# A rotary-embedding kernel: the first slab's load split over two DMA rings, and a second buffer for the sin products

## The chip, the cores and the metric

The kernel runs on one core of a Trainium2 chip. The metric is the device time of one execution in microseconds (us); lower is better. A verdict of faster or slower needs 2%. The profile of a kernel is one execution; its span is about 2 us below the device time.

## The reference

The input x has 16 batches of 512 positions of 16 heads of 64 numbers, all float32; cos and sin have 512 x 32 numbers.

```python
x = x.reshape(batch, seq, num_heads, head_dim)          # 16, 512, 16, 64
x1, x2 = x[..., :half_dim], x[..., half_dim:]
rotated = np.concatenate([x1 * cos - x2 * sin,
                          x1 * sin + x2 * cos], axis=-1)
```

That is 33.5 MB in and 33.5 MB out of HBM, the chip's main memory, with a few operations on each number.

## The kernel before

x is cut into 8 slabs of 2 batches. One slab is a tile in SBUF, the on-chip memory, of 128 partitions, each holding 8192 float32, so one DMA row (one partition) is 32 KB. There are 5 slab buffers. Loads are issued from SP, stores from ScalarE (ACT); each of these two has its own DMA ring, a queue of transfers for the 16 DMA engines (q1 and q10 on the pages below, 33.55 MB each). A slab is worked on in 2 passes: ScalarE casts half a slab to bf16, VectorE (DVE) makes two products and a sum, ScalarE casts the result back into the slab.

```python
slabs = ctx.enter_context(tc.tile_pool(name="slabs", bufs=slots))      # 5
tpool = ctx.enter_context(tc.tile_pool(name="tpool", bufs=3))
t2pool = ctx.enter_context(tc.tile_pool(name="t2pool", bufs=1))
# ... cut
def load(s):
    slab[s] = slabs.tile([P, W], f32, tag="slab", name="slab")
    nc.sync.dma_start(out=slab[s], in_=dram(x, s))

load(0)
# ... cut: cos and sin are loaded through GpSimd, 64 KB each
for s in range(1, slots):
    load(s)
# ... cut: the cos and sin tables are spread with four matmuls
for i, u in enumerate(passes):                 # 16 passes: (slab, half)
    if i + 1 < len(passes):
        cast(passes[i + 1])                    # ScalarE: xb <- slab
    # ... cut
    t2 = t2pool.tile([P, PW], bf16, tag="t2")
    # ... cut: t2 <- xb * sin table; xu <- xb * cos table; xu <- xu + t2  (VectorE)
    nc.scalar.copy(out=view(xs, k * PW, (1, PW)), in_=xu)
    if k == rpp // rows - 1:
        nc.scalar.dma_start(out=dram(out_flat, s), in_=xs)
        if s + slots < nslabs:
            load(s + slots)
```

Of the kernel before, what the change touches and what calls it, by code (L numbers as in the profile page):

```python
# [2 lines left out]

# [4 lines left out]


@with_exitstack  # L10
def kernel(
    ctx: ExitStack,
    tc: tile.TileContext,
    x: bass.AP,
    cos: bass.AP,
    sin: bass.AP,
    num_heads: int,
    out: bass.AP,
):
    nc = tc.nc  # L20
    P = nc.NUM_PARTITIONS

    batch, seq, dim = x.shape
    nh = num_heads
    hd = dim // nh
    half = hd // 2
    bf16 = mybir.dt.bfloat16
    f32 = mybir.dt.float32

    nb = 2  # L30
    slots = 5
    nslabs = batch // nb
    rpp = nb * seq // P
    W = rpp * dim
    SP = seq // rpp
    rows = 4
    PW = rows * dim
    TW = rpp * half

    out_flat = out.rearrange("b s h d -> b s (h d)")  # L40

    singles = ctx.enter_context(tc.tile_pool(name="singles", bufs=1))
    slabs = ctx.enter_context(tc.tile_pool(name="slabs", bufs=slots))
    tpool = ctx.enter_context(tc.tile_pool(name="tpool", bufs=3))
    t2pool = ctx.enter_context(tc.tile_pool(name="t2pool", bufs=1))
    psum = ctx.enter_context(tc.tile_pool(
        name="psum", bufs=1, space=bass.MemoryType.PSUM))


    def dram(t, s, a=0, n=W):  # L50
        return bass.AP(tensor=t.tensor, offset=t.offset + s * nb * seq * dim + a,
                       ap=[[W, P], [1, n]])


    def view(t, offset, *dims):
        return dataclasses.replace(t, offset=t.offset + offset,
                                   ap=[t.ap[0], *[list(d) for d in dims]])


    slab = {}  # L60


    def load(s):
        slab[s] = slabs.tile([P, W], f32, tag="slab", name="slab")
        nc.sync.dma_start(out=slab[s], in_=dram(x, s))  # L65


    load(0)


    TR = seq // P
    G = rpp // TR
    raw = singles.tile([P, 2 * TR * half], f32, tag="raw")
    for i, src in enumerate((cos, sin)):
        nc.gpsimd.dma_start(out=view(raw, i * TR * half, (1, TR * half)), in_=bass.AP(  # L75
            tensor=src.tensor, offset=src.offset,
            ap=[[TR * half, P], [1, TR * half]]))

    for s in range(1, slots):
        load(s)  # L80


    pick = singles.tile([P, G * P], bf16, tag="pick")
    nc.gpsimd.memset(pick, 0.0)  # L84
    for g in range(G):
        part = view(pick, g * P, (SP, P // SP), (1, SP))
        nc.gpsimd.affine_select(  # L87
            out=part, in_=part, compare_op=mybir.AluOpType.not_equal, fill=1.0,
            base=-g, pattern=[[0, P // SP], [-G, SP]], channel_multiplier=1)

    tab1 = singles.tile([P, 2 * TR * half], bf16, tag="tab1")
    nc.vector.tensor_copy(out=tab1, in_=raw)  # L92
    acc = psum.tile([P, 2 * TW], f32, tag="acc")
    for i in range(2):
        for g in range(G):
            nc.tensor.matmul(view(acc, i * TW + g * TR * half, (1, TR * half)),  # L96
                             view(pick, g * P, (1, P)),
                             view(tab1, i * TR * half, (1, TR * half)),
                             start=True, stop=True)

    tab = singles.tile([P, 2 * rpp * hd], bf16, tag="tab")
    nc.vector.tensor_copy(out=view(tab, 0, (hd, 2 * rpp), (1, half)),  # L102
                          in_=view(acc, 0, (half, 2 * rpp), (1, half)))
    nc.vector.tensor_copy(out=view(tab, half, (hd, rpp), (1, half)),  # L104
                          in_=view(acc, 0, (half, rpp), (1, half)))
    nc.vector.tensor_scalar_mul(  # L106
        out=view(tab, rpp * hd + half, (hd, rpp), (1, half)),
        in0=view(acc, TW, (half, rpp), (1, half)), scalar1=-1.0)


    xb = {}


    def cast(u):
        s, k = u
        xb[u] = tpool.tile([P, PW], bf16, tag="xb", name="xb")
        nc.scalar.copy(out=xb[u], in_=view(slab[s], k * PW, (1, PW)))  # L117



    passes = [(s, k) for s in range(nslabs) for k in range(rpp // rows)]
    cast(passes[0])
    for i, u in enumerate(passes):
        if i + 1 < len(passes):
            cast(passes[i + 1])
        s, k = u
        xs, xu = slab[s], xb.pop(u)
        t2 = t2pool.tile([P, PW], bf16, tag="t2")
        for t, a in ((t2, rpp * hd), (xu, 0)):
            nc.vector.tensor_mul(  # L130
                out=t, in0=xu,
                in1=view(tab, a + k * rows * hd, (hd, rows), (0, nh), (1, hd)))
        nc.vector.tensor_add(  # L133
            out=xu, in0=xu,
            in1=view(t2, half, (hd, rows * nh), (-half, 2), (1, half)))
# [8 lines that stand above are left out]
# [1 line left out]
_INS = ['x', 'cos', 'sin', 'num_heads']  # L145
_OUTS = [((16, 512, 16, 64), 'float32')]

_NUMBERS = {'num_heads': 16}


# [26 lines left out]
```

## Time and profile before

| | before |
|---|---|
| device time, first 3 runs | 162.83 us (162.74 to 163.21) |
| span of the profiled run | 160.8 us |
| busy: VectorE, ScalarE | 69%, 71% |
| the two hardware rings, share of 16 DMA engines | 49.3% + 48.3% |
| first slab landed | 13.2 us |
| first store issued | 34.6 us |

The page of the kernel before: the busy line, the share of the 16 DMA engines in 40 slices of the span in tenths, and the DMA queues (packets, MB, share of 16 engines' span). q1 is SP's ring, q10 is ScalarE's, q0 is GpSimd's (POOL). PE is the matrix engine and PEld its weight loads, both nearly idle here.

```profile
PE 0.6 (0%) x4; PEld 0.4 (0%) x4; DVE 111.7 (69%) x52; ACT 114.8 (71%) x33; POOL 2.3 (1%) x9
...
DMA  7999999999999999999999999999999999999993
...
q1 hardware_dynamic: 1152, 33.55, 49.3%
q10 hardware_dynamic: 1152, 33.55, 48.3%
q0 software_dynamic: 64, 0.13, 0.2%
```

The two rings together fill 97.6% of the engines' time, and only the first and last slices fall below 9 tenths. The compute engines have slack of about 30% (busy 69% and 71%). So, by these shares, a change counts only by what it does to DMA work or to the two ends.

The timeline of ScalarE, kernel before (start us, us, engine, line, operation, out<-in, count, and in brackets the idle time before it and its releaser):

```profile
0.74 1.28 ACT L117 ACT_TABLE_LOAD   x1 [0.74 <-PEq L158]
13.25 7.11 ACT L117 CAST xb<-slab 128x4096 bf16<-128x4096 f32 x2 [11.22 <-DMA slab<-in_x_dram]
23.92 3.61 ACT L137 CAST slab<-xb 128x4096 f32<-128x4096 bf16 x1 [3.56 <-DVE xb L133]
...
34.60 0.38 ACTq L139 DMA_DIRECT2D out_dram<-slab  x1
```

ScalarE waits 11.22 us for the first slab. The costliest groups of VectorE (busy us, mean ns of one, then the idle just before them) show that the single sin buffer makes nothing wait, as the sum and the cos product have 0.5 us of idle over 16 passes each:

```profile
L130 DVE TENSOR_TENSOR t<-xb,tab 128x4096 bf16<-128x4096 bf16 x16 | 36.7, 2292 | 19.4 <-ACT xb L117 18.6
L133 DVE TENSOR_TENSOR xb<-xb,t 128x4096 bf16<-128x4096 bf16 x16 | 36.7, 2292 | 0.5
L130 DVE TENSOR_TENSOR xb<-xb,tab 128x4096 bf16<-128x4096 bf16 x16 | 36.7, 2292 | 0.5
```

### The profile page before, as it was taken

Reading aid. Unit: us, or ns where it says so; the run is one execution under the profiler, and the core shown is the slowest. Engines: PE = TensorE matmul, PEld = TensorE weight load, DVE = VectorE, ACT = ScalarE, POOL = GpSimd, SP = SyncE. Lnnn points to the kernel's source line nnn. Section 1 sums busy time; section 2 is a strip of 40 time slices with the busy share of each in tenths; the row PEclk is TensorE's granted clock in tenths of the full one; section 3 lists DMA queues with packets and bytes.
Section 4 is the critical chain, followed back from the end, with each engine's and each line's share of the span. In section 5 each row is a group of like instructions: output and inputs, shape, how many; then the busy total and the mean of one; then the engine's idle time right before and its main releaser. Section 6 shows DMA issues by size and latency. Waiting matters only on the chain.

```text
span 160.8 us, 197 instructions
## 1 busy us (share of the span) xinstructions
PE 0.6 (0%) x4; PEld 0.4 (0%) x4; DVE 111.7 (69%) x52; ACT 114.8 (71%) x33; POOL 2.3 (1%) x9
## 2 busy tenths in 40 slices
PE   0010000000000000000000000000000000000000
PEld 0000000000000000000000000000000000000000
DVE  0012799999999999999997599907997079970000
ACT  3007919999999999999994999069990699926000
POOL 5000000000000000000000000000000000000000
DMA  7999999999999999999999999999999999999993
GB/s 261 408 408 416 497 391 391 505 408 367 416 391 473 440 391 456 457 391 424 489 391 424 489 391 399 514 391 391 522 391 393 489 416 399 481 424 399 481 424 139
DMA packets 2369, 67.25 MB, mean 418 GB/s; under 512 B 288, under 2 KB 288, under 8 KB 320
## 3 DMA queue, kind: packets, MB, share of 16 engines
q1 hardware_dynamic: 1152, 33.55, 49.3%
q10 hardware_dynamic: 1152, 33.55, 48.3%
q0 software_dynamic: 64, 0.13, 0.2%
q14 instruction: 1, 0.01, 0.0%
HBM read 33.69 MB, written 33.55 MB: 418 GB/s over the span
## 4 chain that ended last, share of the span: by engine, by line
DMA 47%; ACT 22%; DVE 21%; issue 0%; ACTq 0%; SPq 0%; DVEq 0%
DMA slab<-in_x_dram 26%; DMA out_dram<-slab 21%; ACT slab L137 11%; ACT xb L117 11%; DVE xb L133 7%; DVE t L130 7%; DVE xb L130 7%; ACTq L137 0%; SPq L65 0%; DVEq L130 0%
## 5 line engine op out<-in xcount | busy, mean ns | idle before, releaser
L117 ACT CAST xb<-slab 128x4096 bf16<-128x4096 f32 x16 | 57.5, 3601 | 24.8 <-DMA slab<-in_x_dram 24.8
L137 ACT CAST slab<-xb 128x4096 f32<-128x4096 bf16 x16 | 57.7, 3604 | 7.2 <-DVE xb L133 7.1
L130 DVE TENSOR_TENSOR t<-xb,tab 128x4096 bf16<-128x4096 bf16 x16 | 36.7, 2292 | 19.4 <-ACT xb L117 18.6
L133 DVE TENSOR_TENSOR xb<-xb,t 128x4096 bf16<-128x4096 bf16 x16 | 36.7, 2292 | 0.5
L130 DVE TENSOR_TENSOR xb<-xb,tab 128x4096 bf16<-128x4096 bf16 x16 | 36.7, 2292 | 0.5
L92 DVE CAST tab<-raw 128x256 bf16<-128x256 f32 x1 | 0.3, 295 | 10.9 <-DMA raw<-in_sin_dram 10.9
L117 ACT ACT_TABLE_LOAD x1 | 1.3, 1283 | 0.7 <-PEq L158 0.7
L102 DVE CAST tab<-acc 128x512 bf16<-128x512 f32 x1 | 0.7, 692 | 0.7 <-PE acc L96 0.7
L75 POOL DMA_DIRECT2D raw<-in_cos_dram x1 | 0.7, 674 | 0.8 <-POOLq L158 0.8
L96 PE MATMUL acc<-tab,pick 128*128 128x128 bf16 x4 | 0.6, 302 | 11.2 <-DVE tab L92 11.2
L87 POOL TENSOR_SCALAR_AFFINE_SELECT pick<-pick 128x128 bf16<-128x128 bf16 x2 | 0.5, 288 | 0.1
L75 POOL DMA_DIRECT2D raw<-in_sin_dram x1 | 0.5, 534 | 0.0
L96 PEld LDWEIGHTS <-pick 128*128 128x128 bf16 x4 | 0.4, 128 | 11.1 <-issue 8.0
L104 DVE CAST tab<-acc 128x256 bf16<-128x256 f32 x1 | 0.4, 414 | 0.0
L106 DVE TENSOR_SCALAR tab<-acc 128x256 bf16<-128x256 f32 x1 | 0.4, 412 | 0.0
L84 POOL MEMSET pick<- 128x256 bf16 x1 | 0.3, 330 | 0.0
L158 POOL MEMSET const-float32-0.0<- 128x1 f32 x1 | 0.1, 99 | 0.2 <-issue 0.2
L158 POOL MEMSET const-uint8-127<- 128x1 uint8 x1 | 0.1, 102 | 0.0
L158 POOL MEMSET const-bfloat16-1.0<- 128x1 bf16 x1 | 0.1, 101 | 0.0
L158 POOL MEMSET const-float32-1.0<- 128x1 f32 x1 | 0.1, 98 | 0.0
## 6 DMA issues: line engine op xcount, KB each, us to landing
slab<-in_x_dram SPq DMA_DIRECT2D x8, 4096.0 KB, 28.2
out_dram<-slab ACTq DMA_DIRECT2D x8, 4096.0 KB, 28.4
raw<-in_cos_dram POOLq DMA_DIRECT2D x1, 64.0 KB, 6.9
raw<-in_sin_dram POOLq DMA_DIRECT2D x1, 64.0 KB, 8.9
```

The lines of the kernel that those rows point to most:

```text
L75: nc.gpsimd.dma_start(out=view(raw, i * TR * half, (1, TR * half)), in_=bass.AP(tensor=src.tensor, offset=src.offset, ap=[[TR * half, P], ...
L84: nc.gpsimd.memset(pick, 0.0)
L87: nc.gpsimd.affine_select(out=part, in_=part, compare_op=mybir.AluOpType.not_equal, fill=1.0, base=-g, pattern=[[0, P // SP], [-G, SP]], c ...
L96: nc.tensor.matmul(view(acc, i * TW + g * TR * half, (1, TR * half)), view(pick, g * P, (1, P)), view(tab1, i * TR * half, (1, TR * half)) ...
L102: nc.vector.tensor_copy(out=view(tab, 0, (hd, 2 * rpp), (1, half)), in_=view(acc, 0, (half, 2 * rpp), (1, half)))
L104: nc.vector.tensor_copy(out=view(tab, half, (hd, rpp), (1, half)), in_=view(acc, 0, (half, rpp), (1, half)))
L106: nc.vector.tensor_scalar_mul(out=view(tab, rpp * hd + half, (hd, rpp), (1, half)), in0=view(acc, TW, (half, rpp), (1, half)), scalar1=-1.0)
L117: nc.scalar.copy(out=xb[u], in_=view(slab[s], k * PW, (1, PW)))
L130: nc.vector.tensor_mul(out=t, in0=xu, in1=view(tab, a + k * rows * hd, (hd, rows), (0, nh), (1, hd)))
L133: nc.vector.tensor_add(out=xu, in0=xu, in1=view(t2, half, (hd, rows * nh), (-half, 2), (1, half)))
L137: nc.scalar.copy(out=view(xs, k * PW, (1, PW)), in_=xu)
L158: nc = _bacc.Bacc("TRN2", target_bir_lowering=False, num_devices=1)
```

## The change

Its intent: VectorE may start the next sin product before the last one is summed, and the first slab, which everything waits for, arrives through both hardware rings. Seven eighths stay on SP's ring, in three DMAs, and every eighth partition goes through ScalarE's ring.

```diff
-    t2pool = ctx.enter_context(tc.tile_pool(name="t2pool", bufs=1))
+    t2pool = ctx.enter_context(tc.tile_pool(name="t2pool", bufs=2))
...
-    load(0)
+    slab[0] = slabs.tile([P, W], f32, tag="slab", name="slab")
+    for q, first, step in ((nc.sync, 0, 2), (nc.scalar, 7, 8),
+                           (nc.sync, 1, 4), (nc.sync, 3, 8)):
+        q.dma_start(
+            out=slab[0][first::step, :],
+            in_=bass.AP(tensor=x.tensor, offset=x.offset + first * W,
+                        ap=[[step * W, P // step], [1, W]]))
```

The four DMAs have 64, 16, 32 and 16 rows of 32 KB.

## The prediction

> **What bounds the kernel now.** The DMA engines. The page's queue lines give 49.3% of 16 engines' span to the load ring and 48.3% to the store ring: 97.6% of 160.8 us. VectorE is busy 69%, ScalarE 71%. A 32 KB row costs an engine 48.3% x 160.8 x 16 / 1024 = 1.213 us on the store ring; on the load ring the mean is 1.239 us, with the slow start in it. The packet records show the two rings' rows taking turns on an engine. Sixteen transfers of 8 rows per engine are 128 x 1.213 = 155.3 us. The rest of the span is the start (first packets at 1.75 to 2.49 us, each engine's first row 1.8 us long), the cos and sin loads, and a tail. The chain of waits runs through ScalarE and VectorE from 13.2 to 63 us, but the rings keep a backlog throughout, so I take DMA as the limit. The last store is issued at 147.5 us; the one before it lands at 150.3.
>
> **Second sin buffer.** [...] one buffer costs nothing: its idle before the product and the sum is 0.5 us in all. The build shows a reorder at the start: ScalarE casts three passes before it writes the first back. The third cast needs slab 1, which lands at 22.9 us; two write-backs of 3.6 us follow, the second after VectorE's second sum at about 30.8: the first store is issued near 34.4 us, as now (34.6). Worth: 0.
>
> **Split load.** Each engine still moves 8 rows of slab 0 first. ScalarE's ring adds no bandwidth: [...] this trace agrees (1.213 us a row with one ring active or two). SP's issue time, 0.4 us per DMA, hides behind 9.7 us per slab. At best the second ring trims the stagger of first packets, under 0.5 us.
>
> There is a cost. [...]
>
> **Prediction.** 162.8 + about 1.2 (half the possible loss): 164.0 us, 8 in 10 between 162.3 and 165.8. Faster by over 2%: 0.01; within 2%: 0.91; slower by over 2%: 0.08.
>
> **What would show it.** The first cast starts at 13.2 us if the split is free, 14.5 to 15.7 with collisions; some rows of 2 to 2.4 us in the first 16 us of packet records; every later event shifted alike; the load ring's share up by about 1%; the first store 21.3 us after the first cast, as now; no change of VectorE's idle before its products.
>
> **What would make it wrong.** [...] the second ring starting all engines earlier (162.3); a changed interleave of loads and stores that leaves a gap before the last store, whose margin is 2.8 us.

The sum came to 164.0 us: 162.8 us, the time of the kernel before, and about 1.2 us, which is half of 2.4 us, the loss on every engine held possible in the two 16-row DMAs, with nothing later to absorb it. That loss was the author's estimate; no trace of the kernel before shows it. "Collisions" stands for longer rows in these two DMAs; the first cast at 14.5 to 15.7 us and the rows of 2 to 2.4 us are forecasts from the same estimate. The idle of 0.5 us in the second paragraph is VectorE's.

The rest can be checked in the trace of the kernel before. The load ring alone, between 20 and 34 us, has rows of 1.217 us on average; the store ring alone, after 150 us, has rows of 1.213 us; together, between 46 and 100 us, they start 361 and 357 rows of 1.214 and 1.213 us. There the taking of turns shows too: 704 of these 718 rows start within 0.005 us of the end of the row 16 places before, and 613 are of the other ring than that row. The records do not name the engine.

## The result, and the profile after

| | before | after |
|---|---|---|
| device time, median of 6 fast runs | 162.74 us (162.29 to 163.21) | 165.11 us (164.84 to 165.22) |
| ratio after / before | | 1.0147 (95%: 1.0125 to 1.0168) |
| span of the profiled run | 160.8 us | 162.9 us |
| first slab landed | 13.2 us | 16.6 us |
| first cast starts | 13.25 us | 17.97 us |
| first store issued | 34.60 us | 38.88 us |

A ratio here is the mean time of one kernel's fast runs over that of the other's fast runs of the same rounds, so it is not quite the ratio of the medians. The change makes the kernel 1.5% slower, which is clear of noise.

The page of the kernel after:

```profile
PE 0.6 (0%) x4; PEld 0.4 (0%) x4; DVE 111.3 (68%) x52; ACT 114.8 (70%) x33; POOL 2.3 (1%) x9
...
DMA  5999899898998998998989989989989899899893
...
q10 hardware_dynamic: 1184, 34.08, 49.0%
q1 hardware_dynamic: 1168, 33.03, 48.5%
q0 software_dynamic: 64, 0.13, 0.3%
```

The same bytes again fill about the same share, but of a longer span: the two rings' packets took 97.6% of 160.8 us, that is 156.9 us per engine, before and 97.5% of 162.9 us, 158.8 us, after. The DMA engines did the same work in more busy time. Half a megabyte has moved from q1 to q10, so the load ring's own share fell.

The same difference in the table of windows (stretch in us, its length, busy time of PE, PEld, DVE, ACT and POOL with counts, granted clock, DMA share, GB/s). The view counts a packet whole in the stretch where it starts, so the share can pass 1, and 16 rows more or less at an edge are 35 GB/s in a stretch of 15 us. First before, then after:

```profile
2.00:17.00 15.00, 0.58 (x4) 0.42 (x4) 1.76 (x5) 3.78 (x3) 1.30 (x4) 1.00 0.95 406
17.00:34.00 17.00, 0.00 (x0) 0.00 (x0) 16.53 (x8) 13.44 (x4) 0.00 (x0) 1.00 1.00 432
34.00:46.00 12.00, 0.00 (x0) 0.00 (x0) 11.66 (x6) 12.00 (x5) 0.00 (x0) 1.00 0.99 399
46.00:150.00 104.00, 0.00 (x0) 0.00 (x0) 81.70 (x36) 84.29 (x24) 0.00 (x0) 1.00 1.00 433
```

```profile
2.00:17.00 15.00, 0.59 (x4) 0.42 (x4) 1.65 (x4) 0.32 (x1) 1.30 (x4) 1.00 1.02 341
17.00:34.00 17.00, 0.00 (x0) 0.00 (x0) 12.32 (x6) 14.96 (x5) 0.00 (x0) 1.00 1.00 432
34.00:46.00 12.00, 0.00 (x0) 0.00 (x0) 11.52 (x6) 11.08 (x5) 0.00 (x0) 1.00 0.98 421
46.00:150.00 104.00, 0.00 (x0) 0.00 (x0) 85.82 (x38) 88.41 (x25) 0.00 (x0) 1.00 1.00 433
```

Look at the last two columns together. In the first stretch the DMA share is near 1 in both, but the rate falls from 406 to 341 GB/s. A row counts as busy for all its length, 2.11 us as well as 1.21 (table below), so the share alone would not have shown it. The third stretch goes the other way, 399 to 421 GB/s, which alone could be an edge (16 rows are 44 GB/s there); the packet records below bear it out.

ScalarE's timeline after:

```profile
0.74 0.57 ACTq L72 DMA_DIRECT2D slab<-in_x_dram  x1
16.68 1.28 ACT L124 ACT_TABLE_LOAD   x1 [16.68 <-DMA slab<-in_x_dram]
17.97 7.11 ACT L124 CAST xb<-slab 128x4096 bf16<-128x4096 f32 x2
26.21 3.60 ACT L124 CAST xb<-slab 128x4096 bf16<-128x4096 f32 x1 [1.13 <-DMA slab<-in_x_dram]
...
38.88 0.35 ACTq L146 DMA_DIRECT2D out_dram<-slab  x1
```

The slab lands 3.4 us later, and the table load of 1.28 us, which stood before the wait, now stands behind it.

The packet records of the two traces give the rest. The table below sorts the 32 KB packets by start and takes them in groups of 16, one group being about one row on each of the 16 engines. It gives the first and last start (us), the ring, and the mean time of a row (us):

```
        before                          after
row     start         ring  mean       start         ring  mean
 1      1.75..2.48    q1    1.780      2.08..2.90    q1    1.803
 2      3.50..3.92    q1    1.236      3.95..4.35    q1    1.237
 3      4.79..5.16    q1    1.213      5.18..5.59    q10   2.109
 4      6.15..6.52    q1    1.213      7.33..8.15    q1    1.493
 5      7.37..7.74    q1    1.213      9.14..9.48    q1    1.215
 6      8.73..9.10    q1    1.218      10.54..10.87  q1    1.267
 7      9.95..10.32   q1    1.216      11.78..12.14  q1    1.218
 8      11.16..11.54  q1    1.215      13.00..13.36  q1    2.172
 9      12.38..12.75  q1    1.217      14.99..15.74  q1    1.691
10      13.59..13.96  q1    1.213      16.86..17.22  q1    1.217
```

Rows 1 to 8 are slab 0. Two of them take 2.1 to 2.2 us instead of 1.21, and the row behind each takes longer too. They stand exactly where the two 16-row DMAs are: row 3 on ScalarE's ring is partitions 7, 15, 23, ..., and row 8 is partitions 3, 11, 19, .... The 16 rows of each start within 0.41 us of one another and take 1.85 to 2.38 us, so all 16 are in flight together (the records do not name the engine). ScalarE's DMA, issued at 0.74 us like SP's, took its turn only third.

The time of an average engine, summed from the same records (us; the 128 rows at 1.213 us, 155.3 us, are the same in all):

| | start of first row | extra in row 1 | extra in rows 2 to 10 | extra in rows 11 to 128 | small packets | end of last row |
|---|---|---|---|---|---|---|
| before | 2.00 | 0.57 | 0.04 | 0.91 | 0.48 | 158.79 |
| after | 2.34 | 0.59 | 2.70 | 0.10 | 0.68 | 161.13 |

The difference at the end is 2.34 us; the columns sum to 2.41 (0.34 + 0.02 + 2.66 - 0.81 + 0.20). With the 155.3 us each line comes to about 0.5 us more than its end, so the records overlap by that much, in both kernels alike. So 2.66 us come from the slow rows of slab 0, 0.34 us from a later start, and 0.81 us are given back later. The experiments ask for the causes.

### The profile page after: what moved, and what is told of

It reads as the page before. It is cut to its first block, busy times and chain, and to the rows that moved or that the text cites. A ratio compares the mean times of both kernels' runs of the same rounds, so it can differ in the third digit from the quotient of the medians.

```text
span 162.9 us, 188 instructions
## 1 busy us (share of the span) xinstructions
PE 0.6 (0%) x4; PEld 0.4 (0%) x4; DVE 111.3 (68%) x52; ACT 114.8 (70%) x33; POOL 2.3 (1%) x9
## 3 DMA queue, kind: packets, MB, share of 16 engines
q1 hardware_dynamic: 1168, 33.03, 48.5%
## 4 chain that ended last, share of the span: by engine, by line
DMA 45%; ACT 25%; DVE 13%; issue 6%; SPq 1%; ACTq 0%
DMA slab<-in_x_dram 25%; DMA out_dram<-slab 21%; ACT slab L144 15%; ACT xb L124 9%; DVE t L137 4%; DVE xb L140 4%; DVE xb L137 4%; ACT L124 1%; SPq L72 1%; ACTq L144 0%; ACTq L124 0%; SPq L65 0%
## 5 line engine op out<-in xcount | busy, mean ns | idle before, releaser
L137 DVE TENSOR_TENSOR t<-xb,tab 128x4096 bf16<-128x4096 bf16 x16 | 36.7, 2292 | 19.6 <-ACT xb L124 19.2
```

What stands on the lines that cost most here:

```text
L137: nc.vector.tensor_mul(out=t, in0=xu, in1=view(tab, a + k * rows * hd, (hd, rows), (0, nh), (1, hd)))
```

## The experiments

The theory, which the expectations below call the collision theory: the two 16-row DMAs cost the time through the set of partitions that they write, and rows written to such a set take up to about twice 1.213 us (2.11 and 2.17 us on average in the trace of the change, 2.38 at most). The rivals: the second ring costs (its first row, the taking of turns); the number of DMAs costs; the new order of work through the second sin buffer costs; the distance between the rows read from HBM costs.

### The second buffer alone

```diff
-    t2pool = ctx.enter_context(tc.tile_pool(name="t2pool", bufs=1))
+    t2pool = ctx.enter_context(tc.tile_pool(name="t2pool", bufs=2))
     ... load(0) as before
```

> The kernel before with the second sin buffer alone. If the split is the whole cause ([...] the second ring, or the number of DMAs): 162.7 us, ratio within 0.3% of 1, slab 0's last landing at 13.2 us as before. If the changed order of casts and write-backs costs (buffer theory): about 165 us, with the first store issued later than 34.6 us though slab 0 lands at 13.2.

Measured: 162.97 us, ratio 0.9995 (0.9957 to 1.0033). The first store was issued at 34.46 us. The second buffer is worth nothing and costs nothing, though it reorders ScalarE's first casts.

### The split alone

```diff
-    t2pool = ctx.enter_context(tc.tile_pool(name="t2pool", bufs=2))
+    t2pool = ctx.enter_context(tc.tile_pool(name="t2pool", bufs=1))
     ... the split load as in the change
```

> The split load with one sin buffer, in the old order of ScalarE's work. Any split theory: 165.1 us, slab 0 landing at 16.6 us. Buffer theory: 162.7 us. ScalarE's table load should again stand after the wait for slab 0.

Measured: 165.29 us, ratio 1.0149 (1.0120 to 1.0178). The split is the whole loss. The 16-row parts' rows took 2.04 and 2.18 us.

### All four DMAs on one ring

```diff
-    ((nc.sync, 0, 2), (nc.scalar, 7, 8),
+    ((nc.sync, 0, 2), (nc.sync, 7, 8),
```

> The change, but the 16-row part of partitions 7, 15, 23, ... is issued on SP's ring like the other three. Collision theory: the two 16-row DMAs keep rows of about 2.1 us plus some spill into the next row, slab 0 lands near 16.5 us, total about 165 us. Ring theory (a ring's first row and the taking of turns between rings cost): landing near 13.5 us, total 162.7 to 163.2 us.

Measured: 164.87 us, ratio 1.0126 (1.0096 to 1.0156). Without the second ring the same two DMAs still have rows of 2.18 and 2.12 us (now the 5th and 8th), and the rows behind them 1.64 us. Extra in rows 2 to 10: 2.78 us. The first stretch of this run's windows has the low rate of the change (347 against 341 GB/s):

```profile
2.00:17.00 15.00, 0.58 (x4) 0.42 (x4) 1.65 (x4) 0.31 (x1) 1.31 (x4) 1.00 1.04 347
```

The second ring is not the cause.

### Both rings, no 16-row DMA

```diff
-    ((nc.sync, 0, 2), (nc.scalar, 7, 8),
-     (nc.sync, 1, 4), (nc.sync, 3, 8))
+    ((nc.sync, 0, 2), (nc.scalar, 3, 4),
+     (nc.sync, 1, 4))
```

> The change with three DMAs: 64 even partitions and 32 on SP, 32 (partitions 3, 7, 11, ...) on ScalarE's ring; no 16-row DMA. Collision theory: [...] rows stay at 1.21 us, landing 13.2 to 13.7 us, total 162.7 to 163.2 us. Ring theory: ScalarE's ring carries twice the bytes, so at least the loss of the change, total 165 us or more. Count theory (each extra DMA costs): about two thirds of the loss, 164.2 us.

Measured: 163.45 us, ratio 1.0031 (1.0001 to 1.0061). Twice the bytes on ScalarE's ring, and every row of slab 0 after the second takes 1.213 to 1.216 us. The windows of this run:

```profile
2.00:17.00 15.00, 0.58 (x4) 0.42 (x4) 1.65 (x4) 3.28 (x2) 1.30 (x4) 1.00 1.04 428
17.00:34.00 17.00, 0.00 (x0) 0.00 (x0) 15.29 (x7) 14.05 (x5) 0.00 (x0) 1.00 1.00 432
34.00:46.00 12.00, 0.00 (x0) 0.00 (x0) 11.48 (x6) 12.00 (x4) 0.00 (x0) 1.00 0.98 390
```

The first stretch has lost nothing (428 GB/s against 341). What is left, 0.3% or 0.5 us (0.0 to 1.0), has room for the later start: the first rows start at 2.28 us on average instead of 2.00.

### Four 32-row DMAs on one ring

```diff
-    for q, first, step in ((nc.sync, 0, 2), (nc.scalar, 7, 8), ...):
+    for q, first, step in [(nc.sync, q, 4) for q in range(4)]:
```

> Slab 0 in four 32-row DMAs, every fourth partition each, all on SP's ring: as many DMAs as the change[...]. Collision theory: rows stay at 1.21 us, total 162.8 to 163.4 us. Count theory (number of DMAs, issues, semaphores): about 165 us.

Measured: 163.53 us, ratio 1.0040 (1.0022 to 1.0058). As many DMAs as in the change, extra in rows 2 to 10 of 0.02 us. The number of DMAs is not the cause of the slow rows. What is left, 0.4% or 0.65 us (0.36 to 0.94), is more than the later start of 0.26 us alone; the mean last row ends 0.43 us later than before, and the rest is not explained.

### Eight 16-row DMAs, and eight of adjacent partitions

The first takes every eighth partition per DMA, the second 16 adjacent partitions.

```diff
-    for q, first, step in ((nc.sync, 0, 2), (nc.scalar, 7, 8), ...):
+    for q, first, step in [(nc.sync, q, 8) for q in range(8)]:
```

> Slab 0 in eight 16-row DMAs, every eighth partition each, all on SP's ring. Collision theory: each row of slab 0 takes up to 2 x 1.213 us, together up to 9.7 us more, slab 0 lands near 23 us, total 170 to 173 us. If a 16-row DMA simply costs a fixed 1.2 us [...]: the same 172 us (the next run, with adjacent partitions, tells these apart).

```diff
+    for q, first in [(nc.sync, 16 * q) for q in range(8)]:
         q.dma_start(
-            out=slab[0][first::step, :],
+            out=slab[0][first:first + 16, :],
             in_=bass.AP(tensor=x.tensor, offset=x.offset + first * W,
-                        ap=[[step * W, P // step], [1, W]]))
+                        ap=[[W, 16], [1, W]]))
```

> Slab 0 in eight 16-row DMAs of 16 adjacent partitions, all on SP's ring: [...] A fixed cost per 16-row DMA: the same time as the strided eight, about 172 us.

Measured: 172.17 us (ratio 1.0574, 1.0556 to 1.0592) for every eighth partition, and 188.48 us (ratio 1.1569, 1.1541 to 1.1596) for adjacent ones. Rows 2 to 8 of slab 0 took 2.37 to 2.56 us in the first, up to 2.1 times 1.213, and 4.41 to 4.60 us in the second, up to 3.8 times. The windows, first every eighth, then adjacent:

```profile
2.00:17.00 15.00, 0.58 (x4) 0.41 (x4) 1.65 (x4) 0.00 (x0) 1.29 (x4) 1.00 1.03 221
17.00:34.00 17.00, 0.00 (x0) 0.00 (x0) 5.10 (x3) 8.88 (x4) 0.00 (x0) 1.00 0.99 347
```

```profile
2.00:17.00 15.00, 0.00 (x0) 0.10 (x1) 0.00 (x0) 0.00 (x0) 1.30 (x4) 1.00 1.00 116
17.00:34.00 17.00, 0.58 (x4) 0.31 (x3) 1.65 (x4) 0.00 (x0) 0.00 (x0) 1.00 0.97 110
```

Adjacent partitions gave about a quarter of the rate (116 and 110 GB/s against 432), every eighth partition about half (221), with the DMA share between 0.97 and 1.03 throughout. A fixed cost per 16-row DMA would have made the two alike. Both have 16 rows per DMA; 16-row DMAs to other sets of partitions were not run.

### Whose step: SBUF's or HBM's?

The two runs above differ on both sides: one reads every eighth row from HBM and writes every eighth partition, the other reads and writes adjacent ones. These two cross the sides. Their outputs are wrong, which doesn't matter for the times. In each expectation the first time is the one forecast if the partitions written set it.

```diff
     # every eighth partition, adjacent rows of HBM
             out=slab[0][first::step, :],
-            in_=bass.AP(tensor=x.tensor, offset=x.offset + first * W,
-                        ap=[[step * W, P // step], [1, W]]))
+            in_=bass.AP(tensor=x.tensor, offset=x.offset + 16 * first * W,
+                        ap=[[W, 16], [1, W]]))
```

> Wrong result on purpose (slab 0's rows are permuted). Eight 16-row DMAs that write every eighth partition, as the strided eight do, but read 16 adjacent rows of HBM. [...] rows of 2.4 to 2.6 us and 172 us, as with every eighth row read. If the distance of the rows read from HBM sets it: rows of about 4.5 us and 188 us, as in the run of adjacent rows.

```diff
     # adjacent partitions, every eighth row of HBM
             out=slab[0][first:first + 16, :],
-            in_=bass.AP(tensor=x.tensor, offset=x.offset + first * W,
-                        ap=[[W, 16], [1, W]]))
+            in_=bass.AP(tensor=x.tensor, offset=x.offset + first // 16 * W,
+                        ap=[[8 * W, 16], [1, W]]))
```

> Wrong result on purpose. Eight 16-row DMAs that write 16 adjacent partitions but read every eighth row of HBM. [...] rows of about 4.5 us, total 188 us. HBM theory: rows of about 2.5 us, total 172 us. Also tells whose step delays the first rows (1.75 us with adjacent rows, 2.09 us with stepped ones).

Measured: 171.82 us (ratio 1.0567, 1.0549 to 1.0584) and 187.85 us (ratio 1.1559, 1.1531 to 1.1587). The first stretch of their windows, every eighth partition first:

```profile
2.00:17.00 15.00, 0.58 (x4) 0.42 (x4) 1.65 (x4) 0.00 (x0) 1.30 (x4) 1.00 1.08 234
```

```profile
2.00:17.00 15.00, 0.00 (x0) 0.10 (x1) 0.00 (x0) 0.00 (x0) 1.29 (x4) 1.00 1.04 122
```

The time goes with the partitions written, not with the rows read. So does the start: with stepped partitions the earliest row began at 2.09 us, with adjacent ones at 1.74 us, whatever was read. That settles on which side the later start arises, though not why: all eight kernels that load slab 0 by stepped partitions begin at 2.06 to 2.09 us, and all those without at 1.74 to 1.75.

### The table load moved out of the way

In every run whose slab 0 is loaded in several DMAs, ScalarE's table load (1.28 us) stands behind the wait for them. This run puts a one-element copy ahead of it.

```diff
+    warm = singles.tile([P, 2], bf16, tag="warm")
+    nc.vector.memset(warm, 0.0)
+    nc.scalar.copy(out=view(warm, 0, (1, 1)), in_=view(warm, 1, (1, 1)))
     TR = seq // P
```

> The change, with a one-element ScalarE copy ahead of the wait for slab 0, so that the table load of 1.28 us is done early. DMA-limit theory: the first cast starts near 16.6 us instead of 18.0, the first store 1.3 us sooner, total unchanged at 165.1 us (within 0.3%). ScalarE-chain theory: 163.8 us.

Measured: 165.21 us, ratio 1.0158 (1.0132 to 1.0183).

```profile
1.35 1.28 ACT L80 ACT_TABLE_LOAD   x1 [1.35 <-PEq L170]
...
16.56 7.11 ACT L129 CAST xb<-slab 128x4096 bf16<-128x4096 f32 x2 [13.72 <-DMA slab<-in_x_dram]
29.30 3.60 ACT L149 CAST slab<-xb 128x4096 f32<-128x4096 bf16 x1 [5.64 <-DVE xb L145]
```

The first cast starts 1.41 us sooner (16.56 against 17.97), and the total does not move. One expectation was missed: the first store came later, at 39.95 us, not sooner, because the order of ScalarE's work changed too. So this run alone does not show what an earlier store would be worth. That the later one did not matter either supports the same reading: work that ScalarE does late at the start is not on the limit while loads keep the DMA engines full.

### The 0.8 us that came back later: two failed attempts

In the kernel before, some load rows around the first store take 1.3 to 1.9 us (0.77 us per engine more than at 1.213 us a row, between 34 and 45 us). The run with the second buffer alone, the one with both rings and no 16-row DMA, and the one with four 32-row DMAs have them too (0.89 to 0.95 us). No kernel with 16-row DMAs has them. In the first group the first store was issued by 36.2 us, in the second at 38.9 us or later, so the moment of the first store was the obvious suspect. These two runs delay the first store of the kernel before by repeating a write-back. (The first expectation puts the slow rows at 1.5 to 2.5 us; in the kernel before they are the 1.3 to 1.9 us above.)

```diff
         nc.scalar.copy(out=view(xs, k * PW, (1, PW)), in_=xu)
+        if (s, k) == (0, 1):
+            nc.scalar.copy(out=view(xs, k * PW, (1, 1400)), in_=view(xu, 0, (1, 1400)))
```

> The kernel before, with one needless partial copy on ScalarE (1400 columns, idempotent) that pushes the first store from 34.6 to about 39.4 us. The runs so far whose first store was issued by 36.2 us have load rows of 1.5 to 2.5 us just ahead of it, 0.8 to 0.95 us per engine in all; those that issued it at 38.9 us or later have none. If the moment of the first store is the cause: no slow rows between 34 and 45 us, total 0.5% below before (about 162.0 us). If the even-paced single load of slab 0 is what goes with the slow rows: they stay, total as before (162.8).

The second one repeats all 4096 columns.

> As the run before it with the whole 4096 columns copied twice, first store near 41.8 us. If the moment of the first store is the cause: no slow rows, about 162.0 us as well, unless the later store uses up the margin of 2.8 us at the end, which would show as idle DMA before the last store. If not: slow rows stay, 162.8 us or more.

Measured: 164.34 us (ratio 1.0085, 1.0067 to 1.0104) with the store at 39.48 us, and 162.83 us (ratio 1.0005, 0.9983 to 1.0026) with the store at 41.89 us. Slow rows stayed with the first store in both; in the first there were more of them between 66 and 78 us (1.0 us per engine). So the moment of the first store is not the cause, and the suspicion is refuted. In all six traces that have slow rows there, the first row over 1.4 us starts 1.1 to 2.4 us after the first store is issued and 1.6 to 3.1 us before that store's own first row. What makes these rows slow, and why they are missing wherever 16-row DMAs loaded slab 0, stays open.

## Why the prediction was right or wrong

- **The DMA engines are the limit: right.** Of the 3.2 us lost in the first 17 us (0.34 + 0.02 + 2.66 + 0.20), all but 0.81 reached the end. With every eighth partition throughout, rows 2 to 10 lost 9.45 us and the kernel took 9.4 us longer. Starting the first cast 1.41 us sooner gained nothing, and a first store 7.3 us later (the second delayed run) cost nothing.
- **The second sin buffer is worth 0: right** (ratio 0.9995). The forecast first store at 34.4 us was 34.46 us in that run, and after the change VectorE's idle before its products is as it was (19.6 and 0.5 us against 19.4 and 0.5).
- **The second ring adds no bandwidth: right.** With 96 rows of slab 0 on SP's ring and 32 on ScalarE's the rows of slab 0 after the second keep 1.213 to 1.216 us, no less than with one ring (1.213 to 1.218 in the kernel before).
- **At best the second ring trims the start by under 0.5 us: it trimmed nothing.** The first rows start later, at 2.34 us on average instead of 2.00, and with all DMAs on one ring at 2.28: it goes with the stepped partitions, not with the ring.
- **"There is a cost": right; its reason was not shown.** It is shown that the two 16-row DMAs cost the time, by taking them away (extra 0.03 and 0.02 us) and by doing all of slab 0 that way (9.45 us in rows 2 to 10), and by the crossed runs that the partitions written set it (171.82 us with every eighth, 187.85 with adjacent ones). Rows took up to 2.1 times 1.213 us with every eighth partition and up to 3.8 times with adjacent ones; no trace shows what in the partitions does that.
- **"About 1.2 (half the possible loss)": the step that was mis-sized.** The prediction halved the loss without a reason from a trace. The rows of such a DMA start within about 0.4 us of each other, and not one of the 32 took under 1.8 us, so every row of both DMAs was slow: 2.66 us per engine instead of 1.2, a little above the 2.4 us that the author gave as the most. It goes above because the rows behind take longer too (1.49 and 1.69 us): the two slow rows alone are 1.86 us over 1.213 each, the two behind them 0.76.
- **That nothing later absorbs the loss: wrong.** 0.81 us were given back in rows 11 to 128, nearly all of it slow rows around the first store that are missing after the change. With the later start of 0.34 and 0.20 us more for small packets the sum came to 2.34 us at the last row, so 165.1 us lay inside the range of 162.3 to 165.8, above the centre of 164.0. That is partly luck: without the 0.81 us, which the prediction had ruled out and whose cause is not known, the same sums give about 165.9 us, just outside.
- **First cast between 14.5 and 15.7 us: wrong, 17.97 us.** The slab landed at 16.59 us, because the loss was full and because its completion came about 0.9 us after its last rows (0.5 us before); the table load added 1.28 us that the prediction had not seen.
- **Every later event shifted alike: wrong.** The first store moved by 4.28 us and the end of the span by 2.1, since loads filled the engines meanwhile. The distance from first cast to first store, 20.9 us, was near the forecast 21.3.
- **The load ring's share up by 1%: wrong.** It fell to 48.5%, as an eighth of slab 0 moved to the other ring and the span grew.

No version here beats the kernel before. The one-DMA load of all 128 partitions is the best of those tried.

## What to carry to other kernels

When a DMA-bound kernel splits a load by partitions, look at the row times of each part in the packet records: parts of 64 and 32 stepped partitions kept full rate in the run that had no others (1.213 to 1.216 us a row after the second), 16 stepped ones ran at about half (mean rows of 2.04 to 2.56 us) and 16 adjacent ones at about a quarter (4.41 to 4.60 us). In these runs the slow parts are all parts of 16 rows, so other sizes need a measurement of their own. The second ring did not help a load that one ring already ran at full rate (ratio 1.0031). Read the DMA share together with GB/s: at 221 GB/s the share was still 1.03, because a slow row counts as busy for all its length.
